# A seven-product form for the down projection of a decoder block, on one core

## The chip, the core and the metric

One Trainium2 chip; the kernel runs on one of its NeuronCores. The metric is the device time of one execution in microseconds, lower is better. In the text PE is TensorE, DVE is VectorE, ACT is ScalarE, POOL is GpSimd and SP is SyncE; POOL and SP issue DMA transfers here.

## The reference

One hybrid block over 528 tokens (16 learned meta tokens and 512 of the input, of which the last 512 are returned): attention and a state-space layer beside each other, an output projection with residual, then a dense feed-forward and a final norm. The part that the change touches, with 2048 features and 5632 = 44 x 128 hidden features:

```
m = rms_norm(h, norm_ffn)
h = h + (silu(m @ w_ffn_gate) * (m @ w_ffn_up)) @ w_ffn_down
out = rms_norm(h, norm_final)
```

All data are float32.

## The kernel before

Activations are held transposed, features on the 128 partitions and tokens along the free dimension. A float32 product runs as three float32r passes: every operand is split into a rounded high part and the remainder, and hi x hi + hi x lo + lo x hi is accumulated in PSUM. So each 128 x 128 weight tile costs three matmuls for each stretch of tokens. `hilo` (L299) makes the two parts, the high one by a copy on ScalarE, the low one by a subtraction on VectorE.

**Weights** come from DRAM in blocks of eight tiles (128 x 1024, 512 KB), loaded on SP's queue by `Weights.load` (L188), and are split in `_split` (L229) in the order of `_items` (L152). An item "P" is a plain block, "S" a unit of the seven-product form, "K" a block that stays in SBUF. `use` (L261) hands out the parts of item i after it has put the splits up to item i + 2 and the combinations (`_combine`, L210) up to item i + 3 into the queues of ScalarE and VectorE. High and low parts have three buffers each.

**Gate and up** are computed for 22 pairs of hidden tiles. Pair 0 is plain (`halves0`, L1275). For pairs 1 to 21, `seven` (L1339) computes two output tiles from 16 K tiles of one matrix as a two-by-two block product (halves of K, of the 512 tokens, and of the pair) in seven units P1, P5, P6, P2, P7, P3, P4 in place of eight. A unit is 8 K tiles x 3 passes = 24 matmuls of 256 columns. Four of the seven weight blocks are combinations made on VectorE, the sums among the products accumulate in the PSUM banks Ra (P1, P6, P7, P4), Rb (P5, P3) and Rc (P2); a unit that continues in a bank starts after the value of the unit before was read from it. The operands of the units are XD (P1), T12 (P5, P6), XA (P2, P3) and T34 (P7, P4); two quartets, gate into Cg and up into Cu, make a pair. Behind a pair VectorE multiplies Cu by Cg (L1397), for pairs 20 and 21 also by the token factor r_h (L1399), and POOL stores it to the DRAM tensor `ad` (L1400).

**Down** has 16 output tiles of 44 K tiles, in three parts of 20, 20 and 4 K tiles (`CHUNKS`, L41). In the first two, `down` (L1405) runs for each output tile 20 x 3 matmuls of 512 columns over streamed plain blocks; the operands are fetched from `ad` on POOL's queue (`fetch`, L1317) into other places, and split from there (`part`, L1331) behind units of the last quartet of gate and up and behind matmuls of the first output tiles. The first part is copied to SBUF (L1474); behind the second, VectorE adds, multiplies by r_h and adds the residual from `hd` (L1478 to L1480). The third part uses weights that stay, for each half of the tokens (L1504 to L1517), between the sums of squares of the final norm; `finish` (L1484) scales and stores.

Each engine works through its queue in the order in which the program issues: a VectorE or ScalarE instruction that waits holds up what is behind it, and so does a DMA issue on POOL or SP.

Of the kernel before, what the change touches and what calls it, by code (L numbers as in the profile page):

```python
# [12 lines left out]
"""  # L13
# [9 lines left out]
F32 = mybir.dt.float32  # L23
# [17 lines left out]
CHUNKS = (range(0, 20), range(20, 40), range(40, 44))  # L41
# [110 lines left out]
def _items():  # L152
    """What the projections take, in order: plain blocks, or (quartet, unit) of the seven-product form."""
# [4 lines left out]
    for q in range(2, 2 * NPAIR):  # L158
        it += [("S", q, u) for u in range(7)]
    d = N_PLAIN + N_GU  # L160
    return it + [("P", d + b) for b in range(80)] + [("K", d + 80 + b, KEEP[b]) for b in range(8)]


class Weights:
    """Weight blocks in the order of their use: loaded ahead, combined, split into hi and lo, handed out."""
# [6 lines left out]
    def __init__(self, nc, pool, ap):  # L172
# [15 lines left out]
    def load(self, upto):  # L188
        """Loads of the items before upto, as far as their places are free."""
# [13 lines left out]
    def _kept(self, tag, i):  # L203
        """The places of a block that stays."""
# [74 lines left out]
def _emit(nc, sp, pp, dp, A, out):  # L279
# [39 lines left out]
    # DRAM scratch  # L319
# [30 lines left out]
    def dense(X, nk, outs):  # L350
        """outs: (psum, first column, last column) of the same weights."""
# [38 lines left out]
    # ------------------------------------------------------------ input norm  # L390
# [52 lines left out]
    # ------------------------------------------------------------ u  # L443
# [873 lines left out]
    def fetch(f, tag, n_=2):  # L1317
# [4 lines left out]
        for i in range(n_):  # L1322
            staged[f + i] = t[:, i, :SEQ]
# [214 lines left out]
```

## Time and profile before

| | |
|---|---|
| Median of 3 runs | 2855.18 us (2852.67 to 2855.69) |
| Span of the profiled execution, first to last instruction | 2849.6 us |
| PE busy | 2816.9 us, 99% of the span |
| VectorE busy | 1668.6 us, 59% |
| ScalarE busy | 1063.2 us, 37% |
| Mean granted TensorE clock | 0.997 of full speed |
| DMA, mean | 120 GB/s, 341 MB |

The profiled execution's own time stands beside the others only as its span; it is 5.6 us (0.2%) under the median of the runs. Times in the rows below are in us from the span's start. Gate and up run to 2341 us, the down stage to 2836 us. A busy time is an engine's own; a row of a timeline merges equal instructions in succession, and an engine's next instruction can start shortly before the record of the one before ends.

### The profile page before, as it was taken

Reading aid. Unit: us, or ns where it says so; the run is one execution under the profiler, and the core shown is the slowest. Engines: PE = TensorE matmul, PEld = TensorE weight load, DVE = VectorE, ACT = ScalarE, POOL = GpSimd, SP = SyncE. Lnnn points to the kernel's source line nnn. Section 1 sums busy time; section 2 is a strip of 40 time slices with the busy share of each in tenths; the row PEclk is TensorE's granted clock in tenths of the full one; section 3 lists DMA queues with packets and bytes.
Section 4 is the critical chain, followed back from the end, with each engine's and each line's share of the span. In section 5 each row is a group of like instructions: output and inputs, shape, how many; then the busy total and the mean of one; then the engine's idle time right before and its main releaser. Section 6 shows DMA issues by size and latency. Waiting matters only on the chain.

```text
span 2849.6 us, 43701 instructions
## 1 busy us (share of the span) xinstructions
PE 2816.9 (99%) x18134; PEld 2524.0 (89%) x18134; DVE 1668.6 (59%) x2262; ACT 1063.2 (37%) x1549; POOL 342.4 (12%) x513
## 2 busy tenths in 40 slices
PE   9999999999999999999999999999999999999997
PEld 8988888889999788888889999999999998888887
DVE  6467457456666433343577777777777783224335
ACT  5223222235555332232344444444444452222124
POOL 2011221221111000111212000000000010000002
PEclk9999999999999999999999999999999999999999
DMA  5344454452222343334434333333333344334332
GB/s 190 105 116 121 126 144 112 132 138 79 68 67 60 115 144 108 114 115 147 138 107 148 122 123 113 125 124 122 119 119 119 134 173 138 96 111 143 108 113 94
DMA packets 103607, 341.41 MB, mean 120 GB/s; under 512 B 14800, under 2 KB 19664, under 8 KB 103344
## 3 DMA queue, kind: packets, MB, share of 16 engines
q1 hardware_dynamic: 76672, 263.36, 28.7%
q0 software_dynamic: 25312, 72.05, 8.7%
q10 hardware_dynamic: 1424, 3.21, 0.5%
q8 instruction: 142, 2.33, 0.3%
q14 instruction: 57, 0.47, 0.1%
HBM read 297.68 MB, written 33.10 MB: 116 GB/s over the span
## 4 chain that ended last, share of the span: by engine, by line
PE 94%; DVE 2%; ACT 1%; issue 1%; DMA 1%; POOL 0%; DVEq 0%; SPq 0%; ACTq 0%; POOLq 0%
PE psA L297 59%; PE psB L297 24%; PE psQ L297 5%; PE psV L297 4%; PE psD L297 2%; DVE ev L304 0%; DVE wlo L244 0%; ACT whi L243 0%; PE psA L1005 0%; DVE H L304 0%; DVE S L301 0%; POOL yd L739 0%; DVE S L304 0%; DMA H<-in_xT 0%; PE psQ L1005 0%
## 5 line engine op out<-in xcount | busy, mean ns | idle before, releaser
L297 PE MATMUL psA<-S,whi 128*128 128x512 f32 (+2 forms) x4960 | 1266.9, 340 | 8.6 <-ACT whi L243 6.3
L297 PEld LDWEIGHTS psA<-S,whi 128*128 128x128 f32 x4960 | 859.1, 188 | 123.3 <-ACT whi L243 6.3
L244 DVE TENSOR_TENSOR wlo<-raw,whi 128x1024 fp32r<-128x1024 f32 (+1 forms) x479 | 592.8, 1239 | 562.1 <-ACT whi L243 560.2
L297 PE MATMUL psA<-S,wlo 128*128 128x512 f32 (+2 forms) x2480 | 841.3, 339 | 0.1
L243 ACT ACTIVATE whi<-raw 128x1024 fp32r<-128x1024 f32 (+1 forms) x479 | 503.9, 1054 | 672.4 <-PE psA L297 324.0
L297 PEld LDWEIGHTS psA<-S,wlo 128*128 128x128 f32 x2480 | 466.8, 188 | 55.3 <-DVE wlo L244 0.5
L297 PE MATMUL psB<-S,whi 128*128 128x256 f32 (+2 forms) x1488 | 353.1, 312 | 0.1
L297 PEld LDWEIGHTS psB<-S,whi 128*128 128x128 f32 x1488 | 255.1, 189 | 17.6 <-PE psD L297 0.3
L297 PE MATMUL psB<-S,wlo 128*128 128x256 f32 (+2 forms) x744 | 231.1, 311 | 0.0
L244 DVE TENSOR_TENSOR wlo<-cmb,whi 128x1024 fp32r<-128x1024 f32 x126 | 154.5, 1226 | 82.5 <-ACT whi L243 82.5
L243 ACT ACTIVATE whi<-cmb 128x1024 fp32r<-128x1024 f32 x126 | 133.0, 1055 | 77.6 <-DVE wlo L244 69.9
L297 PEld LDWEIGHTS psB<-S,wlo 128*128 128x128 f32 x744 | 140.4, 189 | 8.3
L1400 POOL DMA_DIRECT2D ad<-sC x21 | 15.1, 718 | 775.2 <-DVE sC L304 693.8
L817 ACT ACTIVATE ev<-ev 128x512 f32<-128x512 f32 x32 | 20.2, 632 | 151.3 <-DVE ev L304 151.2
L297 PE MATMUL psA<-H,whi 128*128 128x264 f32 (+1 forms) x296 | 73.1, 337 | 1.0 <-DVE ev L304 1.0
L304 DVE TENSOR_TENSOR H<-psA,ev 128x512 f32<-128x512 f32 x32 | 22.1, 691 | 84.9 <-PE psA L297 84.9
L304 POOL TENSOR_TENSOR acc<-acc,ev 128x512 f32<-128x512 f32 (+2 forms) x43 | 53.3, 1240 | 131.3 <-ACT ev L1500 49.7
L301 DVE TENSOR_TENSOR S<-psA,S 128x512 fp32r<-128x512 f32 (+2 forms) x73 | 41.6, 575 | 42.3 <-ACT S L300 42.0
L304 DVE TENSOR_TENSOR ev<-ev,psA 128x512 f32<-128x512 f32 (+1 forms) x18 | 11.9, 659 | 91.0 <-POOL ev L304 88.3
L1368 ACT ACTIVATE ev<-psA 128x256 f32<-128x256 f32 x84 | 31.9, 380 | 86.3 <-PE psA L297 86.3
L297 PE MATMUL psB<-ssA,whi 128*128 128x256 f32 (+1 forms) x276 | 63.7, 319 | 0.0
L297 PE MATMUL psB<-T,whi 128*128 128x256 f32 (+1 forms) x276 | 63.7, 318 | 0.0
(571 smaller groups left out, 4639.3 us busy)
## 6 DMA issues: line engine op xcount, KB each, us to landing
raw<-in_wst SPq DMA_DIRECT2D x485, 512.0 KB, 3.6
ad<-sC POOLq DMA_DIRECT2D x21, 512.0 KB, 3.2
sg<-ev POOLq DMA_DIRECT2D x32, 256.0 KB, 2.3
ev<-sg POOLq DMA_DIRECT2D x32, 256.0 KB, 3.0
H<-ad POOLq DMA_DIRECT2D x11, 512.0 KB, 6.4
U<-ER POOLq DMA_DIRECT2D x64, 64.0 KB, 2.0
ev<-in_xT POOLq DMA_DIRECT2D x16, 256.0 KB, 3.0
hd<-H POOLq DMA_DIRECT2D x16, 256.0 KB, 2.3
```

Of the source, the lines that this page charges most:

```text
L243: self.nc.scalar.activation(hi[:, a:b], w[:, a:b], AF.Copy)
L244: self.nc.vector.tensor_tensor(lo[:, a:b], w[:, a:b], hi[:, a:b], op=ALU.subtract)
L297: PE.matmul(o, lhsT=l, rhs=r, start=start, stop=stop, skip_group_check=more)
L301: DVE.tensor_tensor(lo, src, hi, op=ALU.subtract)
L304: eng.tensor_tensor(o, a, b, op=op)
L817: ACT.activation(e, e, AF.Sigmoid)
L1368: ACT.activation(snap[name], o, AF.Copy)
L1400: POOL.dma_start(ad[2 * pr:2 * pr + 2].rearrange("f p n -> p f n"), Cu)
```

## The change

The token factor r_h is applied to every pair in gate and up, and the four token-side combinations of a pair, which the down projection needs as T12 and T34, are made there (`products`) and stored in a DRAM tensor `td` with the activations. The down projection then takes K tiles 0 to 15, 16 to 31 and 32 to 39 as three parts in the seven-product form (halves of K are even and odd tiles), and the tiles 40 to 43 as before, with weights that stay. In the first two parts the first pair of output tiles is plain (`plain_pair`), the other seven pairs are quartets of seven units; the third part takes four output tiles a quartet, with 4 K tiles and two groups of columns in a unit. The results of units are added straight from PSUM to a buffer C (`added`) that was loaded with the residual (first part) or the partial sum (others), and C goes back to DRAM (`pd`); in the third part it stays in SBUF. The operand tiles of a part are loaded as float32 into their final place and split in place (`begun`, `split`); `change` says behind which unit or plain block each kind is loaded and split, in the last quartet of the part before, the plain pair and the first quartet. The lists of items, the order of weights in DRAM and the tags of the weights that stay follow. Comments are also taken out.

```diff
-CHUNKS = (range(0, 20), range(20, 40), range(40, 44))
+DCH = (range(0, 16), range(16, 32), range(32, 40))
+LAST = range(40, 44)
...
+N_DOWN = (32, 32, 16)
-KEEP = ("ssB", "ER", ("S8", "S9"), ("S10", "S11"), ("S12", "S13"), ("S14", "S15"), ("v", "w"), ("U", "KS"))
+KEEP = ("ER", ("v", "w"), ("S0", "S1"), ("S2", "S3"), "ssA", "ssB", ("S8", "S9"), ("S10", "S11"))
...
-    return it + [("P", d + b) for b in range(80)] + [("K", d + 80 + b, KEEP[b]) for b in range(8)]
+    for c, n in enumerate(N_DOWN):
+        for q in range(n // 4):
+            if q == 0 and c < 2:
+                it += [("P", d + b) for b in (0, 2, 1, 3)]
+            else:
+                it += [("S", d + 4 * q, u) for u in range(7)]
+        d += n
+    return it + [("K", d + b, KEEP[b]) for b in range(8)]
...
+    def products(pr, Cu, T12_, T34_):
+        POOL.dma_start(td[pr, 0:2].rearrange("f p n -> p f n"), Cu)
+        if pr >= LAST.start // 2:
+            return
+        a, b = Cu[:, 0], Cu[:, 1]
+        tt(T12_[:, lo_], a[:, hi_], a[:, lo_], SUB)
+        tt(T34_[:, lo_], b[:, hi_], a[:, hi_], SUB)
+        tt(T12_[:, hi_], b[:, hi_], T12_[:, lo_], SUB)
+        tt(T34_[:, hi_], b[:, lo_], T12_[:, hi_], SUB)
+        POOL.dma_start(td[pr, 2], T12_)
+        POOL.dma_start(td[pr, 3], T34_)
...
+        tt(a, a, r_h, MUL)
+    products(0, Cu, ev(SEQ), ev(SEQ))
...
+    def added(C, nm):
+        def done(name, o):
+            for n_, m, c in {"P1": ((0, 0, lo_),), "P2": ((0, 0, lo_),), "P5": ((0, 1, hi_),), "P7": ((0, 1, hi_),),
+                             "P6": ((0, 0, hi_),), "P3": ((0, 0, hi_),), "P4": ((0, 1, lo_),)}[name]:
+                t = C[m][:, :, c]
+                tt(t, t, o.rearrange("p (m n) -> p m n", m=nm), ADD)
+        return done
+    def begun(tag, part, src, pair=None):
+        t = slot(tag, part)
+        if pair is None:
+            POOL.dma_start(t[:, 1].bitcast(F32), src)
+            return t
+        POOL.dma_start(t[:, 1].bitcast(F32).rearrange("p (k n) -> p k n", k=2), src.rearrange("k p n -> p k n"))
+        return t
+    def split(t):
+        ACT.activation(t[:, 0], t[:, 1].bitcast(F32), AF.Copy)
+        tt(t[:, 1], t[:, 1].bitcast(F32), t[:, 0], SUB)
...
+    def change(N):
+        L, S = (lambda kind, *k: lambda: N.load(kind, k)), (lambda kind, *k: lambda: N.split(kind, k))
+        if N.n == 8:
+            last = {"P1": [L("XD", 0, 1, 2, 3)],
+                    "P6": [S("XD", 0, 1, 2, 3), L("B12", 0, 1, 2, 3), L("T12", 0, 1, 2, 3)],
+                    "P7": [S("B12", 0, 1)],
+                    "P3": [S("B12", 2, 3), L("XA", *range(8))],
+                    "P4": [S("XA", 0), L("T34", *range(8))]}
+            plain = [[S("XA", 1, 2, 3, 4)], [S("XA", 5, 6, 7), L("T12", 4, 5, 6, 7)],
+                     [S("T12", 0, 1, 2, 3), S("T34", 0)], [S("T12", 4, 5, 6, 7)]]
+            first = {"P1": [S("T34", 1, 2, 3)], "P5": [S("T34", 4, 5)], "P6": [S("T34", 6)], "P2": [S("T34", 7)]}
+        else:
+            last = {"P1": [L("XD", 0, 1)],
+                    "P6": [S("XD", 0, 1), L("T12", 0, 1, 2, 3)],
+                    "P7": [S("T12", 0, 1)],
+                    "P3": [S("T12", 2, 3), L("XA", 0, 1, 2, 3)],
+                    "P4": [L("T34", 0, 1, 2, 3)]}
+            plain = None
+            first = {"P1": [S("XA", 0, 1, 2, 3)], "P5": [S("T34", 0, 1)], "P6": [S("T34", 2, 3)]}
+        return last, plain, first
...
-        if 2 * pr >= CHUNKS[2].start:
-            tt(Cu, Cu, rb, MUL)
-        POOL.dma_start(ad[2 * pr:2 * pr + 2].rearrange("f p n -> p f n"), Cu)
+        tt(Cu, Cu, rb, MUL)
+        products(pr, Cu, Cg[:, 0], Cg[:, 1])
+    def preload(c, m):
+        t = sb([P, 2, SEQ], F32, ("H7", "sC")[m % 2])
+        POOL.dma_start(t, (hd, pd[0])[c][2 * m:2 * m + 2].rearrange("k p n -> p k n"))
+        cbuf[c, m] = t
+    for c in range(2):
+        N = parts[c]
+        nxt_last = changes[c + 1][0]
+        for m in range(8):
...
+            if m == 0:
...
+                for j, o in enumerate(plain_pair(N.X, plain)):
+                    tt(C[:, j], C[:, j], o, ADD)
+            else:
+                hooks = {k: list(v) for k, v in (changes[c][2] if m == 1 else nxt_last if m == 7 else {}).items()}
+                hooks["P1"] = hooks.get("P1", []) + pre
+                C = cbuf.pop((c, m))
+                seven(N.X, 8, 1, added([C[:, 0:1], C[:, 1:2]], 1), hooks)
+            POOL.dma_start(pd[c][2 * m:2 * m + 2].rearrange("k p n -> p k n"), C)
...
+    N = parts[2]
+    hload(0)
+    hload(1)
+    for q in range(4):
+        hooks = {k: list(v) for k, v in (changes[2][2] if q == 0 else {}).items()}
+        if q == 0:
+            hooks["P3"] = [act_load]
+        elif q == 2:
+            for i, n_ in enumerate(("P1", "P6", "P7", "P4")):
+                hooks[n_] = [lambda i=i: act_split(i)]
+        if q < 3:
+            hooks.setdefault("P2", []).extend([lambda: hload(2 * q + 2), lambda: hload(2 * q + 3)])
+        seven(N.X, 4, 2, added(h2s[2 * q:2 * q + 2], 2), hooks)
```

`hload` loads two tiles of the second part's sums from `pd` into the places where the result stays; `act_load` and `act_split` do for the tiles 40 to 43 what `begun` and `split` do; `plain_pair` runs four plain blocks, the first two over XD and B12 (48 matmuls of 256 columns each), the others over XA (24 of 512). Loads of XD and B12 take 256 of the 512 columns of two tiles.

## Rows read from the trace of the kernel before

**Rows 1.** The page's head: the span, and for each engine busy us, share of the span and number of instructions.

```profile
span 2849.6 us, 43701 instructions
PE 2816.9 (99%) x18134; PEld 2524.0 (89%) x18134; DVE 1668.6 (59%) x2262; ACT 1063.2 (37%) x1549; POOL 342.4 (12%) x513
```

**Rows 2.** All waits of PE from 1290 us (output projection) to 2340 us (end of gate and up): us in total, times, longest.

```profile
PE psD L297 <- ACT whi L243: 0.8, 1, 0.8
PE psD L297 <- DVE wlo L244: 0.8, 1, 0.8
PE psA L297 <- DVE sC L304: 0.6, 1, 0.6
```

**Rows 3.** The table by stretch: from, to, length; busy us (and instructions) of each engine; granted clock; mean share of the DMA engines; GB/s. The first stretch is one pair of gate and up, the second the start of the down stage, the third the rest of its first part, the fourth most of its second part.

```profile
2224.00:2263.30 39.30, 39.30 (x338) 39.30 (x338) 30.58 (x31) 18.10 (x23) 0.72 (x1) 1.00 0.36 121
2341.00:2380.00 39.00, 39.00 (x170) 31.50 (x169) 19.88 (x24) 15.24 (x23) 6.60 (x11) 1.00 0.71 257
2380.00:2564.00 184.00, 184.00 (x793) 148.72 (x792) 48.39 (x47) 49.40 (x60) 2.05 (x4) 1.00 0.32 100
2640.00:2787.00 147.00, 147.00 (x636) 118.86 (x635) 51.95 (x56) 30.56 (x29) 4.31 (x8) 1.00 0.35 111
```

**Rows 4.** The chain that ended last, merged: start, us, engine, tile, instructions. The same step of two quartets of the seven-product form, with twelve between them.

```profile
1786.87 5.65 PE psA L297 x48
...
2042.45 5.64 PE psA L297 x48
```

**Rows 5.** PE's timeline (start, us of the merged run, engine, line, operation, tiles, count): the first matmuls of the down stage and the first of its last part.

```profile
2340.87 0.64 PE L297 MATMUL psA<-v,whi 128*128 128x512 f32 x2
...
2786.85 0.76 PE L297 MATMUL psA<-T,keep 128*128 128x256 f32 x5
```

**Rows 6.** PE's timeline in the last part: the first and the last of seven runs of six matmuls in a row.

```profile
2798.95 0.87 PE L297 MATMUL psA<-ssA,keep608S 128*128 128x256 f32 x6
...
2803.21 0.88 PE L297 MATMUL psB<-ssA,keep609S 128*128 128x256 f32 x6
```

**Rows 7.** VectorE's timeline (in brackets: idle time before it and what ended it): behind the first pair of gate and up, behind pair 19 and behind pair 20.

```profile
1516.27 2.49 DVE L304 TENSOR_TENSOR S<-H,S 128x512 fp32r<-128x512 f32 x4
1518.68 1.22 DVE L244 TENSOR_TENSOR wlo<-cmb,whi 128x1024 fp32r<-128x1024 f32 x1
...
2263.14 1.22 DVE L244 TENSOR_TENSOR wlo<-cmb,whi 128x1024 fp32r<-128x1024 f32 x1
...
2301.32 1.23 DVE L304 TENSOR_TENSOR sC<-sC,H 128x1024 f32<-128x1024 f32 x1 [0.56 <-ACT sC L1376]
2302.58 1.23 DVE L304 TENSOR_TENSOR sC<-sC,rstd 128x1024 f32<-128x1024 f32 x1
2303.72 1.22 DVE L244 TENSOR_TENSOR wlo<-cmb,whi 128x1024 fp32r<-128x1024 f32 x1
2304.86 1.22 DVE L224 TENSOR_TENSOR raw<-raw,raw 128x1024 f32<-128x1024 f32 x1
```

**Rows 8.** VectorE's timeline in the last part: additions from PSUM (512 and 256 columns), and at the end two operations of 256 of which the second needs the first.

```profile
2787.05 0.69 DVE L304 TENSOR_TENSOR H<-H,psB 128x512 f32<-128x512 f32 x1 [9.52 <-PE psB L297]
...
2791.39 0.41 DVE L304 TENSOR_TENSOR H<-H,psA 128x256 f32<-128x256 f32 x1
2791.72 0.41 DVE L304 TENSOR_TENSOR H<-H,psB 128x256 f32<-128x256 f32 x1
...
2836.80 0.89 DVE L304 TENSOR_TENSOR ev<-ev,S 128x256 f32<-128x256 f32 x2 [0.48 <-ACT S L384]
```

**Rows 9.** The timeline of PE's weight loads: the first low part of P6 behind the first pair and behind pair 20.

```profile
1520.07 0.19 PEld L297 LDWEIGHTS psA<-S,wlo 128*128 128x128 f32 x1
...
2306.47 0.19 PEld L297 LDWEIGHTS psA<-S,wlo 128*128 128x128 f32 x1
```

**Rows 10.** VectorE's timeline in the last quartet of gate and up: a pair of splits, and the addition of P7.

```profile
2333.51 1.28 DVE L301 TENSOR_TENSOR S<-wraw,S 128x512 fp32r<-128x512 f32 x2
...
2337.39 0.41 DVE L304 TENSOR_TENSOR sC<-ev,psA 128x256 f32<-128x256 f32 x1
```

**Rows 11.** PE's timeline there: the first matmuls of P4.

```profile
2337.94 0.48 PE L297 MATMUL psA<-S,whi 128*128 128x256 f32 x2 [0.60 <-DVE sC L304]
```

**Rows 12.** POOL's timeline at the start of the down stage: two issues of loads, of 512 and of 256 KB.

```profile
2352.60 0.72 POOL L1321 DMA_DIRECT2D sC<-ad  x1 [1.64 <-DMA ad<-sC]
2353.32 0.56 POOL L1321 DMA_DIRECT2D acc<-ad  x1
```

**Rows 13.** DMA issues: tiles, queue, operation, count, KB each, median us from issue to landing.

```profile
H<-ad POOLq DMA_DIRECT2D x11, 512.0 KB, 6.4
...
sC<-ad POOLq DMA_DIRECT2D x5, 512.0 KB, 4.2
```

**Rows 14.** The table by stretch, columns as in rows 3, in three stretches of 5 us at the start of the down stage.

```profile
2340.00:2345.00 5.00, 5.00 (x27) 4.24 (x26) 4.96 (x7) 3.23 (x6) 1.43 (x2) 1.00 1.01 395
2345.00:2350.00 5.00, 5.00 (x23) 4.02 (x23) 5.00 (x9) 4.30 (x7) 2.15 (x3) 1.00 1.02 395
2350.00:2355.00 5.00, 5.00 (x23) 4.05 (x22) 3.52 (x4) 1.06 (x1) 3.10 (x6) 1.00 0.99 360
```

More of the change, by code (lines that the diff above doesn't have):

```diff
@@ L324, in _emit @@
     hd = dp.tile([KT, P, SEQ], F32, name="hd")
-    ad = dp.tile([NFT, P, SEQ], F32, name="ad")
+    td = dp.tile([NPAIR, 4, P, SEQ], F32, name="td")
+    pd = [dp.tile([KT, P, SEQ], F32, name=f"pd{i}") for i in range(2)]
     gv = sb([P, 56], F32, "gv")
@@ L1328, in _emit @@
-    STAGE = {0: "wraw", 2: "wraw", 4: "wraw", 6: "H0", 8: "H1", 10: "H2", 12: "H6", 14: "H3", 16: "H0", 18: "H1",
-             20: "H2", 22: "H6", 24: "H3", 26: "H0"}
-    def part(f):
-        acts[f] = slot(*slots[f % 28])
-        hilo(acts[f][:, 0], acts[f][:, 1], staged.pop(f))
-        st.done.add(("act", f))
-        if f in range(7, 18, 2):
-            fetch(f + 9, STAGE[f + 9])
-    def seven(C, last):
-        Ra, Rb, Rc = ps([P, 512], "A")[:, :H2], ps([P, 512], "B")[:, :H2], None
-        snap = {}
-        for u, name in enumerate(UNITS):
+    X = {"XD": XD, "XA": XA, "T12": T12, "T34": T34}
@@ L1361, in seven @@
-            if last:
-                for f in PART.get(name, ()):
-                    part(f)
-                for f in FETCH.get(name, ()):
-                    fetch(f, STAGE[f])
+            for m in range(nm):
+                om = o[:, m * H2:(m + 1) * H2]
+                for k in range(nk):
+                    c = (m * nk + k) * P
+                    wh, wl = hi[:, c:c + P], lo[:, c:c + P]
+                    x = X["XD"][k // 2][:, :, k % 2] if name == "P1" else \
+                        X[{"P5": "T12", "P6": "T12", "P7": "T34", "P4": "T34"}.get(name, "XA")][k]
+                    if name != "P1":
+                        x = x[:, :, hi_ if name in ("P3", "P6", "P4") else lo_]
+                    start = m == k == 0 and name in ("P1", "P5", "P2")
+                    mm(om, wh, x[:, 0], start, False, True)
+                    mm(om, wh, x[:, 1], False, False, True)
+                    mm(om, wl, x[:, 0], False, k == nk - 1, True)
@@ L1366, in seven, with gathered @@
+            for h in hooks.get(name, ()):
+                h()
+            done(name, o)
+        seven_n[0] += 1
+    def gathered(C):
+        snap = {}
+        def done(name, o):
             if name in ("P1", "P5", "P6"):
@@ new lines, in _emit, with __init__, load, split @@
+    class Operands:
+        def __init__(self, c):
+            self.i0, self.n = DCH[c].start // 2, len(DCH[c]) // 2
+            self.raw, self.X = {}, {n: [None] * self.n for n in ("XA", "T12", "T34")}
+            self.X["XD"], self.X["B12"] = [None] * (self.n // 2), [None] * (self.n // 2)
+        def load(self, kind, ks):
+            for k in ks:
+                i = self.i0 + (2 * k if kind in ("XD", "B12") else k)
+                if kind in ("XD", "B12"):
+                    tag, part = (NX[8 + k] if kind == "XD" else (f"S{4 + k}", 0))
+                    t = begun(tag, part, td[i:i + 2, 0][:, :, lo_ if kind == "XD" else hi_], 2)
+                else:
+                    tag, part = {"XA": NX[k], "T12": (f"S{k}", 0), "T34": (f"S{8 + k}", 0)}[kind]
+                    t = begun(tag, part, td[i, {"XA": 1, "T12": 2, "T34": 3}[kind]])
+                self.raw[kind, k] = t
+        def split(self, kind, ks):
+            for k in ks:
+                t = self.raw.pop((kind, k))
+                split(t)
+                self.X[kind][k] = k2(t) if kind in ("XD", "B12") else t
@@ L1379, in _emit @@
     seven_n = [0]
-    PART = {"P5": range(0, 2), "P6": range(2, 4), "P2": range(4, 6), "P7": range(6, 8), "P3": range(8, 10),
-            "P4": range(10, 12)}
-    FETCH = {"P6": (8, 10), "P2": (12,), "P7": (14,)}
+    parts = [Operands(c) for c in range(3)]
+    changes = [change(N) for N in parts]
     rb = r_h.unsqueeze(1).to_broadcast([P, 2, SEQ])
@@ L1391, in _emit @@
         Cu = sb([P, 2, SEQ], F32, "sC")
[L1392 to L1405 removed]
+        seven(X, 8, 1, gathered(Cu), changes[0][0] if pr == NPAIR - 1 else {})
@@ new lines, in _emit, with hload, act_load, act_split @@
+    hs_, h2s = [], []
+    def hload(j):
+        t = sb([P, 2, SEQ], F32, f"S{(4, 5, 6, 7, 12, 13, 14, 15)[j]}")
+        POOL.dma_start(t, pd[1][2 * j:2 * j + 2].rearrange("k p n -> p k n"))
+        h2s.append(t)
+        hs_.extend([t[:, 0], t[:, 1]])
+    acts, begun_ = {}, {}
+    def act_load():
+        for i, f in enumerate(LAST):
+            begun_[f] = begun(*NX[(6, 7, 10, 11)[i]], td[f // 2, f % 2])
+    def act_split(i):
+        f = LAST[i]
+        split(begun_[f])
+        acts[f] = begun_[f]
@@ L1406, in down @@
+    def down(fs, ot, c, w):
         p = ps([P, 512], "AB"[ot % 2])
```

161 lines of the change are left out of this document (59 added, 102 removed).

## The prediction

> **What bounds the kernel now.** The page's list of busy times comes first: PE is busy 99% of the span, VectorE 59%, ScalarE 37% [rows 1]. A busy PE is not yet a PE that nothing holds up, so the waits of PE come next: from the output projection to the end of gate and up (1,050 us) three waits, 2.2 us together [rows 2]. The table by stretch then tells what each stage does beside PE: gate and up keep VectorE busy 30.58 of 39.3 us, the down stage only 48.39 of 184 us; the granted clock is 1.00 (2.4 GHz) in both, and DMA is used to a third [rows 3]. So the kernel ends when PE has pushed its columns through; VectorE in gate and up has some 8 us of slack in a pair of products, and in the down stage much.
>
> Two paces give the prices. Units of the seven-product form repeat on the chain of waits every 19.66 us: 13 periods from 1786.87 to 2042.45, each of 168 matmuls of 256 columns, 117.0 ns apiece [rows 4]. A unit of 24 is then 2.81 us. The first two parts of the down stage run from 2340.87 to 2786.85, 445.98 us for 32 output tiles of 60 matmuls of 512 columns: 13.94 us a tile, 232.3 ns a matmul [rows 5].
>
> **The gain.** Those two parts hold 40 K tiles by 16 output tiles. After the change they are 20 blocks of 16 K tiles by two output tiles (or 8 by four): 2 in plain form, 18 in seven products. A plain pair now costs 96 matmuls of 256 and 48 of 512 columns, 96 x 117.0 + 48 x 232.3 ns = 22.38 us; a seven costs 19.66. 18 x 19.66 + 2 x 22.38 = 398.6 us, **47.3 us less** than 445.98. Sevens of the third part use chains of four K tiles; the trace has chains of four in the last stage, 36 matmuls from 2798.95 to 2803.21, 118.3 ns [rows 6]. The ends are 117.0 and 118.3, at most 0.9 us over 672 matmuls; I take 117.0, since the seven's order of operands is kept.
>
> The Trainium skill (TensorE: Matmul & The Clock Gate, section "Wait — 56ns, not 53.3ns?") gives a warm matmul N / 2.4 GHz plus about 2.5 ns, a fixed cost that speaks against more and shorter matmuls. By it, 109.2 and 215.8 ns, an estimate, a seven would save 2.4 us in place of 2.6 and the gain would be 42.6 us. The rows show 117.0 and 232.3 ns, so the measured overhead grows with the columns, and the rows decide.
>
> **What is added beside PE.** In a seven of the down stage VectorE has 7 low parts and 4 combinations, which start 1.14 us apart back to back [rows 7], and 7 additions from PSUM of 0.41 us [rows 8]: at most 2.70 us in a unit, 15.4 of 19.66. It fits in 2.81, so I cost it at nothing. In the third part the additions are 512 wide, 0.69 us [rows 8]: 2.97 us in four units and 1.83 in three, 17.4 in all, which the slack of two units ahead takes up. Without that cover each addition would stand on the path, 2.9 us a quartet. Weight blocks are as many as before, on SP's queue; stores and reloads of partial sums add 1 MB a quartet on POOL's, which only issues there. The three additions and multiplications per output tile of the old second part were hidden [rows 3] and return nothing.
>
> **Where stalls come in.** (a) *Products in each pair.* Behind Cu, VectorE now multiplies by the token factor and takes four differences before the low part that the next quartet's P6 wants. Pair 20 shows the multiplication already: Cu*Cg at 2301.32, the factor at 2302.58, low part at 2303.72 [rows 7]. Small operations of 256 start 0.33 apart when independent and 0.45 when one needs the other [rows 8]: first difference at 2303.84, the others at 2304.17, 2304.50 and 2304.95, low part at 2305.28, done 2306.50. PE loads that low part at 2306.47 [rows 9], and a signal takes 0.1: PE resumed at 2337.94 after an addition from 2337.39 that lasted 0.41 [rows 10, 11]. So 0.14 us a pair, 19 pairs: **2.7 us**; ends 0 and 0.45 a pair, 8.5 us. POOL's three stores come behind it and gate Cg's place only at the next P2, 8 us on.
> (b) *First pair.* There the low part for P6 follows four splits at 1516.27 and ends at 1519.90 [rows 7], PE wants it at 1520.07 [rows 9]. One factor (0.7) and four differences (1.5) come ahead: 2.2 - 0.17 + 0.1 = **2.1 us**, ends 0 and 3.
> (c) *Gate and up into the first part.* Before, 12 tiles were split in that last quartet (two of 0.64 us a unit [rows 10]), and PE waited 0.6 [rows 11]. Now nine are, with loads one unit or more ahead, but the copy of P6 stands behind four splits on ScalarE. I put 1.0 in place of 0.6: **0.4**. The plain pair follows, with two weight blocks already split (11 us), so a late XA0 holds VectorE and not PE. The same cover serves the step from the first part to the second. In each first seven VectorE has seven splits more, 15.4 + 7 x 0.6 = 19.6 us: I get 0.2 late at P7, **0.4** for both.
> (d) *Second part into the third.* No plain pair here. POOL issues four T34 loads behind P4 (0.56 each), the store of C and then the first two loads of partial sums (0.72 each [rows 12]): the first is issued 2.96 us after P4. A 512 KB load landed 6.4 us after issue in the crowded stretch and 4.2 outside [rows 13]; the crowd is nearer. It lands at 9.4, VectorE adds P1 by 10.1, and P6, which accumulates into that bank, starts at 10.2 where it wanted 5.6: 4.6 us. Behind that addition stand two combinations, two low parts, four splits and two additions, 8.3 us, to 18.4; P7 needs the last at 15.8: 2.7 more. **7.3 us**; with 4.2 it is 5.1, with all landed early 0, with a landing two us later 10.
>
> **Sum.** -47.3 + 2.7 + 2.1 + 0.4 + 0.4 + 7.3 = -34.4 us. On the profiled span, 2849.6, that gives 2815.2. The runs' median, 2855.18, lies 5.6 above that span and carries what surrounds it; I leave that difference as it is: **2820.8 us**.
>
> **The rivals.** *Covers hold.* The steps (a) to (d) cost under 6 us: 2808 to 2814. For it: PE lost only 0.6 us in the old change of operands, which split more tiles in a quartet [rows 10, 11]. Against: no old step put a load from DRAM in front of an addition that PE waits for.
> *Transfers too slow at the full changes.* A full change fetches 32 tiles of 256 KB (8.4 MB), half of those for XD and B12 in rows of 1 KB, beside weights of 100 GB/s [rows 3] and 1.6 MB of partial sums. XD's 1.0 MB comes early; from P6 of one quartet to P7 of the quartet behind the plain pair PE has some 42 us for the rest: 7.4 + 1.6 + 4.2 = 13.2 MB, 314 GB/s. At a full DMA share the trace moved 360 to 395 GB/s [rows 14], which suffices; 257, the mean of the old change [rows 3], would take 51 us, 9 late at each of two changes: 2839.
> The Trainium skill (DMA: Bandwidth & Descriptors, section "Where 436 GB/s comes from") puts a core's share of HBM at about 358 GB/s. The rows passed it here, 395 GB/s; by 358 the bytes would still fit, an estimate of 37 us.
> *The chain of products has no cover: slower.* If the factor and the four differences (1.26 + 1.56 = 2.82 us) were wholly on the path of each pair, 19 x 2.82 = 53.6 us in place of 2.7: 2872. It decides from 2.4 us a pair. For it: VectorE runs without a gap from Cu to that low part [rows 7]. Against: the low part was ready 2.8 us early in pair 19 (2263.14 + 1.22 against 2267.15, a period before 2306.47) and 1.5 early in pair 20, and 0.14 is what is left of it.
> *The third part gains nothing.* Its quartets take the plain time (short chains, wide additions): 4 x 2.6 = 10.5 us back, 2831.
>
> **How the numbers follow.** Forecast 0.55 (2814 to 2828), covers hold 0.15, slow transfers 0.20, no gain in the third part 0.04, chain without cover 0.06. The predicted time is the forecast's. The range runs from 2808 (covers hold) to 2841 (slow transfers), and leaves out the slower case and some of both tails. About 0.2%, 5.7 us, is what a measurement tells from no change: faster takes the first four cases but for 0.02 of the slow transfers that would end near 2855; slower is the chain.
>
> **What would show it.** Right: sevens of 19.7 us in the down stage, the matmuls' last stage beginning some 34 us earlier in all, pairs of gate and up at 39.3 to 39.5 us, a PE wait on VectorE at P6 and P7 in the first quartet of the third part, DMA near full share at three places. Wrong: pairs above 40 us (a), sevens above 20.5 us in the middle of a part (additions on the path), PE waiting on ScalarE or VectorE for splits in a plain pair (transfers), or a granted clock below 1.00 in the down stage, which would mean that waits are longer than reckoned.

## The result and the profile after

The changed kernel takes **2831.2 us** (median of 4 runs, 2828.9 to 2832.3) against 2853.9 for the kernel before beside it: ratio 0.992, 95% interval 0.9906 to 0.9934, 22.7 us less. Forecast were 2820.8 (34.4 less) in a range of 2808 to 2841. The profiled spans differ by 19.3 us, 2849.6 and 2830.3. The head of the page, answering to [rows 1]: PE 35 us less, VectorE 240 us more.

```profile
span 2830.3 us, 47269 instructions
PE 2781.7 (98%) x19526; PEld 2566.1 (91%) x19526; DVE 1908.8 (67%) x2609; ACT 1136.6 (40%) x1625; POOL 413.5 (15%) x633
```

Starts of stages, from PE's timeline (start, us, engine, line, operation, tiles, count), in this order: pairs 20 and 21 of gate and up, its last quartet; the plain pair, the first and the second seven of part 1; the same three of part 2; the first two quartets of part 3; the last part.

```profile
2265.35 0.40 PE L314 MATMUL psA<-v,whi 128*128 128x256 f32 x2
...
2304.80 0.28 PE L314 MATMUL psA<-v,whi 128*128 128x256 f32 x1
...
2324.46 0.40 PE L314 MATMUL psA<-v,whi 128*128 128x256 f32 x2
...
2344.12 0.40 PE L314 MATMUL psA<-v,whi 128*128 128x256 f32 x2
...
2366.71 0.40 PE L314 MATMUL psA<-v,whi 128*128 128x256 f32 x2
...
2395.73 0.40 PE L314 MATMUL psA<-v,whi 128*128 128x256 f32 x2
...
2513.99 0.40 PE L314 MATMUL psA<-v,whi 128*128 128x256 f32 x2
...
2536.57 0.39 PE L314 MATMUL psA<-v,whi 128*128 128x256 f32 x2
...
2565.60 0.40 PE L314 MATMUL psA<-v,whi 128*128 128x256 f32 x2
...
2683.56 0.40 PE L314 MATMUL psA<-v,whi 128*128 128x256 f32 x2
...
2709.68 0.40 PE L314 MATMUL psA<-v,whi 128*128 128x256 f32 x2
...
2768.50 0.88 PE L314 MATMUL psA<-T,keep 128*128 128x256 f32 x6
```

A pair of gate and up lasts 39.45 us (39.32 before), its last quartet 19.66. The plain pairs last 22.59 and 22.58 us (2344.12 to 2366.71, 2513.99 to 2536.57). The sevens in the middle of a part last 19.66: from 2395.73 to 2513.99 it is 118.26 for six, 0.3 over six times that. But the first sevens of parts 1 and 2 last **29.02 and 29.03** (2366.71 to 2395.73, 2536.57 to 2565.60), and the first quartet of part 3 lasts 26.12. In what PE waited for in the down stage, those three stand out (PE's timeline, the wait in brackets; P6 of the first sevens, then P6 in part 3):

```profile
2379.47 0.77 PE L314 MATMUL psA<-S,whi 128*128 128x256 f32 x2 [4.05 <-DVE sC L321]
2548.71 0.77 PE L314 MATMUL psA<-S,whi 128*128 128x256 f32 x2 [4.03 <-DVE sC L321]
2693.05 0.77 PE L314 MATMUL psA<-S,whi 128*128 128x256 f32 x2 [3.70 <-DVE S L321]
```

Each wait is followed by slow matmuls. The table by stretch (columns as in rows 3) for the first change of operands and the seven behind it:

```profile
2345.00:2370.00 25.00, 25.00 (x167) 22.84 (x167) 17.33 (x22) 10.83 (x17) 8.11 (x14) 1.00 1.02 392
...
2370.00:2375.00 5.00, 3.66 (x21) 2.48 (x19) 2.22 (x4) 2.76 (x5) 0.00 (x0) 1.00 0.32 125
2375.00:2380.00 5.00, 0.95 (x4) 0.77 (x5) 5.00 (x8) 3.63 (x7) 0.90 (x2) 0.72 0.28 105
2380.00:2385.00 5.00, 5.00 (x29) 5.00 (x28) 5.00 (x7) 2.00 (x3) 0.56 (x1) 0.59 0.69 202
2385.00:2390.00 5.00, 5.00 (x44) 5.00 (x43) 4.63 (x7) 2.22 (x3) 0.00 (x0) 1.00 0.34 112
```

DMA is at full share for 25 us, at 392 GB/s; [rows 14] had 360 to 395 for 15 us. Then PE stands, and in the 5 us after the wait the granted clock is 0.59, near the lower of its two levels (1.2 GHz, the other is 2.4): 29 matmuls in place of 44. So the 9.4 us that the first seven of part 1 is too long are three things: P5 ends 3.1 us late, PE waits 4.05 us for P6, and P6 takes 2.3 us longer than elsewhere. What PE stood for is read backwards. VectorE's timeline (start, us, ..., in brackets the idle time before):

```profile
2359.34 1.23 DVE L241 TENSOR_TENSOR cmb<-raw,raw 128x1024 f32<-128x1024 f32 x1 [5.31 <-DMA raw<-in_wst]
2360.48 1.22 DVE L261 TENSOR_TENSOR wlo<-raw,whi 128x1024 fp32r<-128x1024 f32 x1
2361.61 3.09 DVE L321 TENSOR_TENSOR S<-S 128x512 fp32r<-128x512 f32 x5
...
2374.17 0.69 DVE L321 TENSOR_TENSOR S<-S 128x512 fp32r<-128x512 f32 x1 [0.77 <-ACT S L1413]
2374.78 0.68 DVE L321 TENSOR_TENSOR H<-H,psA 128x512 f32<-128x512 f32 x1
2375.38 0.68 DVE L321 TENSOR_TENSOR H<-H,psB 128x512 f32<-128x512 f32 x1
2375.97 1.22 DVE L261 TENSOR_TENSOR wlo<-cmb,whi 128x1024 fp32r<-128x1024 f32 x1
2377.11 1.89 DVE L321 TENSOR_TENSOR S<-S 128x512 fp32r<-128x512 f32 x3
2378.92 0.41 DVE L321 TENSOR_TENSOR sC<-sC,psA 128x256 f32<-128x256 f32 x1
```

The addition of P1 at 2378.92, which P6 waits for, stands behind three T34 splits, a low part, the sums of the plain pair and the last T12 split at 2374.17. That split waited for ScalarE, and ScalarE for four landings:

```profile
2368.22 0.63 ACT L1413 ACTIVATE S<-S 128x512 fp32r<-128x512 f32 x1 [6.02 <-DMA S<-td]
2370.73 0.63 ACT L1413 ACTIVATE S<-S 128x512 fp32r<-128x512 f32 x1 [1.88 <-DMA S<-td]
2372.04 0.63 ACT L1413 ACTIVATE S<-S 128x512 fp32r<-128x512 f32 x1 [0.67 <-DMA S<-td]
2373.51 0.63 ACT L1413 ACTIVATE S<-S 128x512 fp32r<-128x512 f32 x1 [0.84 <-DMA S<-td]
```

Those are T12 4 to 7. POOL issued them behind the XA loads, which begin at 2339.68, behind all eight T34 loads (the fifth of them at 2349.22), a store and a load of a buffer C (POOL's timeline, T12 4 to 7 last):

```profile
2339.68 1.07 POOL L1407 DMA_DIRECT2D ssA<-td  x2 [2.31 <-PE psB L314]
...
2349.22 1.20 POOL L1407 DMA_DIRECT2D S<-td  x2 [2.25 <-DMA ER<-td]
...
2356.02 0.57 POOL L1407 DMA_DIRECT2D S<-td  x1 [0.78 <-PE psB L314]
2356.82 0.55 POOL L1407 DMA_DIRECT2D S<-td  x1 [0.24 <-issue]
2358.13 0.54 POOL L1407 DMA_DIRECT2D S<-td  x1 [0.76 <-DMA S<-td]
2359.59 0.54 POOL L1407 DMA_DIRECT2D S<-td  x1 [0.92 <-DMA S<-td]
```

Their places S4 to S7 hold B12 until the second block of the plain pair has read it, but tile by tile, and the issues come 3.8 to 4.6 us after that: the block's matmuls on the four tiles of B12 end at 2351.4, 2352.9, 2354.3 and 2355.7. POOL was still at what stands ahead in its queue; the view's `PE psB` at 2356.02 is the last semaphore to move, not the end of that place's use (experiment 1 shows the same issues coming as each place falls free). P5 begins at 2369.5 (2366.71 + 2.81) and wants the last of them 21 matmuls later, at 2372.0; its split ends at 2374.9.

In part 3 the addition of P1 itself stands, for the partial sums:

```profile
2692.22 0.69 DVE L321 TENSOR_TENSOR S<-S,psA 128x512 f32<-128x512 f32 x1 [3.15 <-DMA S<-pd]
```

Other steps. Behind pair 19 VectorE now runs (answering to [rows 7]):

```profile
2265.96 1.23 DVE L321 TENSOR_TENSOR sC<-sC,H 128x1024 f32<-128x1024 f32 x1 [0.56 <-ACT sC L1390]
2267.22 1.23 DVE L321 TENSOR_TENSOR sC<-sC,rstd 128x1024 f32<-128x1024 f32 x1
2268.48 0.76 DVE L321 TENSOR_TENSOR H<-sC 128x256 f32<-128x256 f32 x2
2269.16 0.88 DVE L321 TENSOR_TENSOR H<-sC,H 128x256 f32<-128x256 f32 x2
2269.95 1.22 DVE L261 TENSOR_TENSOR wlo<-cmb,whi 128x1024 fp32r<-128x1024 f32 x1
```

The low part is done at 2271.2, and the first low matmul of P6 behind it starts 2271.23. On the chain of waits, P6 behind a pair takes 2.94 us, P6 in the middle of a pair 2.83 (start, us, engine, tile, instructions):

```profile
1541.48 2.83 PE psA L314 x24
...
1561.14 2.94 PE psA L314 x24
```

### The profile page after: what moved, and what is told of

Its sections match the earlier page's. It is cut to its first block, busy times and chain, and to the rows that moved or that the text cites. A ratio compares the mean times of both kernels' runs of the same rounds, so it can differ in the third digit from the quotient of the medians.

```text
span 2830.3 us, 47269 instructions
## 1 busy us (share of the span) xinstructions
PE 2781.7 (98%) x19526; PEld 2566.1 (91%) x19526; DVE 1908.8 (67%) x2609; ACT 1136.6 (40%) x1625; POOL 413.5 (15%) x633
## 3 DMA queue, kind: packets, MB, share of 16 engines
q10 hardware_dynamic: 1424, 3.21, 0.5%
## 4 chain that ended last, share of the span: by engine, by line
PE 92%; DVE 3%; DMA 3%; issue 1%; ACT 1%; POOL 0%; DVEq 0%; SPq 0%; POOLq 0%; ACTq 0%
PE psA L314 60%; PE psB L314 19%; PE psQ L314 6%; PE psV L314 5%; DMA S<-td 2%; PE psD L314 1%; DVE S L321 1%; DVE wlo L261 1%; DVE ev L321 0%; PE psA L1023 0%; ACT whi L260 0%; DMA ER<-td 0%; DMA H<-in_xT 0%; PE psQ L1023 0%; PE psB L678 0%
## 5 line engine op out<-in xcount | busy, mean ns | idle before, releaser
L314 PE MATMUL psA<-S,whi 128*128 128x256 f32 (+2 forms) x5472 | 1317.9, 328 | 20.5 <-DVE sC L321 8.1
L314 PEld LDWEIGHTS psA<-S,whi 128*128 128x128 f32 x5472 | 930.8, 189 | 119.1 <-ACT S L1413 8.5
L314 PE MATMUL psA<-S,wlo 128*128 128x256 f32 (+2 forms) x2736 | 896.9, 328 | 2.6 <-DVE wlo L261 2.6
L314 PE MATMUL psB<-S,whi 128*128 128x256 f32 (+1 forms) x1424 | 293.5, 284 | 2.4 <-DVE S L321 1.4
L261 DVE TENSOR_TENSOR wlo<-cmb,whi 128x1024 fp32r<-128x1024 f32 x180 | 219.8, 1221 | 68.4 <-ACT whi L260 67.3
L314 PE MATMUL psB<-S,wlo 128*128 128x256 f32 (+1 forms) x712 | 200.3, 281 | 0.0
L241 DVE TENSOR_TENSOR cmb<-raw,raw 128x1024 f32<-128x1024 f32 x60 | 73.1, 1219 | 11.4 <-DMA raw<-in_wst 11.4
L241 DVE TENSOR_TENSOR cmb<-cmb,raw 128x1024 f32<-128x1024 f32 x60 | 73.2, 1219 | 0.0
L241 DVE TENSOR_TENSOR raw<-raw,raw 128x1024 f32<-128x1024 f32 x60 | 73.1, 1218 | 0.0
L241 DVE TENSOR_TENSOR cmb<-raw,cmb 128x1024 f32<-128x1024 f32 x60 | 73.1, 1218 | 0.0
```

The costliest lines, as they stand in the source:

```text
L241: self.nc.vector.tensor_tensor(t, g(a), g(b), op=op)
L261: self.nc.vector.tensor_tensor(lo[:, a:b], w[:, a:b], hi[:, a:b], op=ALU.subtract)
L314: PE.matmul(o, lhsT=l, rhs=r, start=start, stop=stop, skip_group_check=more)
```

## Experiments

Theory A: at a full change DMA is full, T12 4 to 7 are issued last on POOL's queue and land last, and everything behind their splits is late. B: VectorE has too much to do in a first seven. C: the bytes are too many in whatever order. Diffs are against the changed kernel, for the last five against the kernel named. Lengths of the three slow stages are in the table behind.

**1. T34 4 to 7 behind T12 4 to 7.**

```diff
-"P4": [S("XA", 0), L("T34", *range(8))]}
+"P4": [S("XA", 0), L("T34", 0, 1, 2, 3)]}
-[S("XA", 5, 6, 7), L("T12", 4, 5, 6, 7)],
+[S("XA", 5, 6, 7), L("T12", 4, 5, 6, 7), L("T34", 4, 5, 6, 7)],
```

> Changed kernel, but T34's tiles 4 to 7 are loaded behind T12's tiles 4 to 7 (after the second plain block) and not before them. Theory A (T12 4 to 7 land late because they stand behind eight T34 loads in POOL's queue while DMA is full, and ScalarE and VectorE wait for them in order): the first seven of parts one and two falls from 29.0 us to 20 to 24 us each, the kernel to 2813 to 2822 us. Theory B (VectorE has too much to split and add in a first seven): 28 to 29.5 us each, no change. Theory C (too many bytes in the window, whatever their order): now T34 comes late, 27 to 30 us each.

2824.1 us. First sevens 23.0 and 24.7 us in place of 29.0: 10.3 us come back with the same bytes and the same work. That is A. Of the 10.3 us, 8.2 come back before P6 begins and 4.4 in P6, which now runs at the full clock; 2.2 go again at P7. Waits of 1.67 and 1.17 us stay in the first, 3.40 and 1.16 in the second. POOL now issues T12 4 to 7 as their places fall free, one tile of B12 after the other (its timeline; the last row has two T34 loads with T12 7):

```profile
2353.98 0.57 POOL L1407 DMA_DIRECT2D S<-td  x1 [1.80 <-PE psB L314]
2355.41 0.55 POOL L1407 DMA_DIRECT2D S<-td  x1 [0.86 <-PE psB L314]
2356.85 0.54 POOL L1407 DMA_DIRECT2D S<-td  x1 [0.88 <-PE psB L314]
2358.26 1.60 POOL L1407 DMA_DIRECT2D S<-td  x3 [0.87 <-PE psB L314]
```

Counted from the start of the plain pair (2346.37 here, 2344.12 in the changed kernel) they are issued 3.5 to 4.3 us earlier and land 4.9 to 6.1 us earlier. So most of the gain is an earlier issue, the rest a shorter way from issue to landing.

**2. T34 of parts 1 and 2 not fetched.** The old tiles are split again, so P7 and P4 of those parts multiply old operands.

```diff
+ if kind == "T34" and self.n == 8:
+     self.raw[kind, k] = (parts[0].X if self.i0 else X)["T34"][k]
+     continue
```

> Changed kernel without the reload of T34 in parts one and two: its old tiles are split again in place, so all work of ScalarE, VectorE and PE stays and 4 MB of transfers go (the products with T34 then have old operands). Theories A and C: first sevens of 19.7 to 21 us in place of 29.0, the kernel near 2812 us. Theory B: 28 to 29.5 us, no change.

2819.5 us; first sevens 22.2, where 19.7 to 21 was forecast, and 20.3. With 2 MB less to fetch in each change and every split still there, 2.5 and 0.7 us over 19.66 remain: B can't be more than that.

**3. First two loads of partial sums for part 3 behind P2** of the last quartet of part 2.

```diff
+ if c == 1 and m == 7:
+     hooks["P2"] = hooks.get("P2", []) + [lambda: hload(0), lambda: hload(1)]
...
-    hload(0)
-    hload(1)
     for q in range(4):
```

> Changed kernel, but the first two loads of partial sums for the third part are issued behind P2 of the last quartet of part two, not behind the T34 loads. Theory (the addition of P1 waits for that load): the first seven of part three falls from 26.1 us to 20 to 22 us, the kernel by 4 to 6 us. Rival (the splits of XA and T34 in front of the additions hold PE): 25 to 26 us, no change. The first sevens of parts one and two stay at 29.0 us.

2825.6 us. The first quartet of part 3 lasts 23.1 in place of 26.1, at a clock of 1.00; the wait at P6 fell from 3.70 to 0.67 us, and a second one of 2.33 us at P7, which waits for VectorE's addition of P6, took its place. So step (d) had both its mechanisms; in the changed kernel the second was covered by slow matmuls. The 23.1 lies between the two forecasts. And of the 5.6 us less in the whole the edit itself accounts for 3.0: the first sevens of parts 1 and 2 come before it and last 27.4 and 27.8 here. That is how far one profile of the same code can differ from another; experiment 4 has 28.1 and 27.4. Against those, experiment 1 gained 7.5 and 7.8 us in place of 10.3.

**4. Products of a pair behind P1 of the next pair.**

```diff
-        seven(X, 8, 1, gathered(Cg), {})
+        seven(X, 8, 1, gathered(Cg), {"P1": [lambda: products(pr - 1, Cu, Cg[:, 0], Cg[:, 1])]})
...
-        products(pr, Cu, Cg[:, 0], Cg[:, 1])
```

> Changed kernel, but stores and differences of a pair are issued behind P1 of the next pair's gate quartet, so behind the low part for P6 (the factor stays where it is). Theory (a low part that comes 0.14 us late in each pair, 2.6 us late in the first): pairs of gate and up fall from 39.44 to 39.32 us, the first quartet of pair 1 from 24.0 to 19.7 to 20.7 us, the kernel by 5 to 7 us. Rival (the work only moves on and meets the next low part or the additions): pairs stay at 39.4 us or more, the kernel within 2 us.

2830.4 us, where 5 to 7 less was forecast. Pairs last 39.32 in place of 39.45, so step (a) is shown, and the first quartet of pair 1 lasts 20.1; but pair 1 begins 5.7 us later in this profile than in the changed kernel's, and 2.4 us are less than one run can tell in the whole.

**5. Additions ahead of the splits.**

```diff
+            done(name, o)
             for h in hooks.get(name, ()):
                 h()
-            done(name, o)
```

> The changed kernel with one swap: in every unit the value of the unit is read (the addition into C) before the splits that the unit's hook issues, in place of behind them. Loads and their order stay. Theory A with VectorE's order (late T12 tiles, and then three T34 splits of 1.9 us in VectorE's queue ahead of the addition of P1 that P6 waits for): the last T12 split is as late as before, but the wait at P6 shrinks from 4.05 us to some 2.1, and if the granted clock then stays at 1.00 the 2.5 us of slow matmuls go too: first sevens of parts 1 and 2 of 24.5 to 27.2 us each against 29.0, first quartet of part 3 by its four XA splits (2.7 us) from 26.1 to 22 to 24, the whole 2817 to 2825 us. Rival, landing alone: the splits wait for the landings whatever the order, first sevens stay at 28.5 to 29.5, 2829 to 2833. Rival, order made worse: an addition that waits for PE now holds up the splits behind it and P7 or P2 waits in turn: over 2833.

2831.7 us (2829.3 to 2833.7, 4 runs; ratio to before 0.992, 0.9908 to 0.9938): no gain. The waits at P6 did fall, from 4.05 and 4.03 to 2.25 each, and the first sevens to 26.5 and 27.7; but part 3's first quartet grew to 29.5, since the addition of P1, now first, waits for the partial sums and holds the XA splits behind it (4.35 us at P6, then 1.99 at P7, clock 0.66 after either). The rival of a worse order holds there, A's arithmetic in the first sevens.

**6. Edits 1, 3 and 4 together.**

> Three edits together: T34 4 to 7 loaded behind T12 4 to 7, the first two loads of partial sums for part 3 behind P2 of the last quartet of part 2, and the products of a pair issued behind P1 of the next pair. By the stretches measured one at a time against the changed kernel: first sevens 23.0 and 24.7 in place of 29.0 each (-10.3), first quartet of part 3 23.1 in place of 26.1 (-3.0), pairs 39.32 in place of 39.45 (19 x 0.13 = -2.4), first quartet after pair 0 20.1 in place of 24.0 (-3.9): -19.6, so some 2811.5 us (2808 to 2815). Rival (the gains overlap: VectorE or DMA that one edit relieves is what the other edit relied on): 2816 to 2822.

2818.0 us (2817.1 to 2822.0; ratio 0.9878, 0.9863 to 0.9892). It misses 2811.5: the first sevens keep their gain (23.3, 24.5), part 3 gives half (24.6, with the wait of 2.32 us followed by a clock of 0.71), and the 3.9 us on the first pair were not there to be had: five kernels that issue it as the changed one does waited 0.41, 0.41, 1.70, 2.15 and 2.58 us at that place. (This profile gains 4.1 us there, but its pair 1 begins 2.8 us later than the changed kernel's.) The trace shows what is left in the first seven: VectorE stands before the first combination, then runs without a gap.

```profile
2349.02 1.29 DVE L321 TENSOR_TENSOR T<-T 128x512 fp32r<-128x512 f32 x2
2356.10 1.23 DVE L241 TENSOR_TENSOR cmb<-raw,raw 128x1024 f32<-128x1024 f32 x1 [5.80 <-DMA raw<-in_wst]
```

So the weight blocks on SP's queue are late as well in the crowd, and with them the T12 splits that are queued behind the combination and were long landed.

**7. Edits 1, 3, 4 and 5.**

> The three edits of the run before and the values of units read before the hook's splits. If VectorE's order is what is left at P6 of the first sevens (1.67 us, and 3.40 at the second change) and at P7 of part 3 (2.33), those waits lose up to 1.9, 1.9 and 2.0 us: 2806 to 2809. If the landings alone set them: within 1.5 us of the run before.

2818.7 us (2818.4 to 2822.3; 0.9881, 0.9865 to 0.9898): as the run before, where up to 12 us less was forecast if VectorE's order were what is left. The first addition no longer waits for splits but for its buffer, `sC<-hd`, which POOL loads last of all (VectorE's timeline):

```profile
2371.29 0.42 DVE L321 TENSOR_TENSOR sC<-sC,psA 128x256 f32<-128x256 f32 x1 [1.55 <-DMA sC<-hd]
```

**8. As 7, all eight T34 loads behind T12 4 to 7.**

> As the run before, but all eight T34 tiles are loaded behind T12 4 to 7 and split behind the first seven's units. Theory A (order in POOL's queue with DMA full): the last T12 tiles land 4 loads (1 MB, 2.6 us at 395 GB/s) earlier, so the waits at P6 of both first sevens go, each seven 19.7 to 21 us, 1 to 4 us less than the run before. Theory C (the bytes do not fit): T34 lands too late in turn, P7 waits as long as P6 did, no gain or a loss of 1 to 3 us.

2820.2 us (2819.1 to 2821.5; 0.9883, 0.9868 to 0.9898): no gain. VectorE stands 3.21 us ahead of the same addition (1.55 in the run before), whose buffer is now loaded behind four more tiles (the view names no releaser; by the trace the buffer lands at 2373.85 and the addition starts at 2373.93), PE waits 2.69 at P6, and T34 is late in turn (0.95 and 0.96 at P7).

**9. As 6, T12 0 to 3 split a block earlier**, and T34 2 and 3 of part 3 split behind P2.

```diff
-[S("XA", 5, 6, 7), L("T12", 4, 5, 6, 7), ...
+[S("XA", 5, 6, 7), S("T12", 0, 1, 2, 3), L("T12", 4, 5, 6, 7), ...
-[S("T12", 0, 1, 2, 3), S("T34", 0)], ...
+[S("T34", 0)], ...
-"P5": [S("T34", 0, 1)], "P6": [S("T34", 2, 3)]}
+"P5": [S("T34", 0, 1)], "P2": [S("T34", 2, 3)]}
```

> The kernel with three edits (2818.0 us), and: the splits of T12 0 to 3 stand behind the second block of the plain pair in place of the third, and T34 2 and 3 of part 3 are split behind P2 in place of P6. In the three-edit kernel VectorE stands idle for 5.8 us behind the XA splits, until a weight block lands that the first combination of the first seven needs (DMA full), and then runs without a gap to the end of the first seven. Theory D (weights late on SP's queue hold VectorE's queue, and what is behind it is late by as much): the four splits (2.5 us) fall into that idle time, and the wait at P6 of the first seven (1.99 us) goes to 0.5 or less, first sevens 20.5 to 22 and 23 to 24.5, whole 2813.5 to 2816.5. Rival E (C of the first seven, loaded last on POOL's queue, lands just as late): P6 waits for that load in place of VectorE, first sevens as before within 0.7 us. Part 3: addition of P6 is 1.28 us earlier, wait at P7 2.32 down to 1.0 to 1.3.

2818.7 us (2817.3 to 2823.5; 0.9878, 0.9863 to 0.9893): no gain. The splits did fall into the idle time (3.14 left of 5.80), and the first seven is as long as before, since the addition of P1 now waits for the buffer C (0.96 us of the 1.86 that PE waits). The second is 1.0 us longer (25.4). Part 3 went as forecast: 22.8 in place of 24.6, a wait of 1.12 at P7 (and one of 0.58 in it). Rival E holds for the first seven:

```profile
2373.26 0.42 DVE L321 TENSOR_TENSOR sC<-sC,psA 128x256 f32<-128x256 f32 x1 [0.96 <-DMA sC<-hd]
```

**10. As 9, C of the first seven loaded ahead of T34 4 to 7.**

```diff
-                plain[2] += pre
+                plain[1][-1:-1] = pre
```

> As the run before, and the load of C for the first seven is issued ahead of T34 4 to 7. If rival E holds: the wait at P6 goes here, first sevens 20.0 to 21.5 and 22 to 23.5, 1.5 to 4 us less than the run before. If theory D alone holds: no change, or 1 us more because T34 6 and 7 land later.

2816.4 us (2814.4 to 2817.4; 0.9866, 0.9851 to 0.9881). First seven 22.0, wait at P6 0.67 in place of 1.86, as E has it. The second is no shorter (25.9), where 22 to 23.5 was forecast: there T12 4 to 7 land 12.2 to 12.9 us after their issue, their splits end at 2529.9, and 4 us of VectorE's work (sums of the plain pair, a low part, three T34 splits) stand between these and the addition of P1 at 2533.96. That is a wait of 3.37 us and a clock of 0.50 after it.

**11. As 10, all T34 loaded last, additions ahead of splits.**

> As the run before, but all eight T34 tiles are loaded last, and a unit's value is read before the hook's splits. At the second change T12 4 to 7 still landed 10 us after issue with T34 0 to 3 ahead of them (wait at P6 3.0). If order decides there: second first seven 21 to 22 in place of 23, whole up to 2 us less than the run before. If the bytes decide: T34 makes P7 and P4 wait 1 to 2.4 us, as in the earlier run with T34 last (0.25 and 0.95, 1.43 and 0.96), whole 0 to 2 us more.

**2813.5 us** (2811.8 to 2819.0; 0.986, 0.9844 to 0.9877), the lowest median, though its runs overlap with those of experiment 10 and the two profiled spans are both 2812.6. First sevens 20.9 and 21.6 us; these are two edits at once, and how much of the 4.3 us in the second is the order of the loads and how much that of the additions was not separated. What the sevens gain is in part lost elsewhere: 25.1 for 22.8 in the first quartet of part 3 (waits of 1.98 and 1.18 at P7, where additions ahead of splits had cost time in experiment 5 too) and 21.4 for 19.8 in that of pair 1. Of the waits in the first sevens three are left, 2.4 us in all (sum, times, longest):

```profile
PE psA L314 <- DVE S L321: 1.9, 2, 0.9
PE psA L314 <- DVE sC L321: 0.5, 1, 0.5
```

| kernel | first seven, part 1 | part 2 | first quartet, part 3 | us |
|---|---|---|---|---|
| changed | 29.0 | 29.0 | 26.1 | 2831.2 |
| 1 T12 first | 23.0 | 24.7 | 26.0 | 2824.1 |
| 2 no T34 | 22.2 | 20.3 | 26.5 | 2819.5 |
| 3 sums early | 27.4 | 27.8 | 23.1 | 2825.6 |
| 4 products later | 28.1 | 27.4 | 27.5 | 2830.4 |
| 5 additions first | 26.5 | 27.7 | 29.5 | 2831.7 |
| 6 = 1, 3, 4 | 23.3 | 24.5 | 24.6 | 2818.0 |
| 7 = 6 and 5 | 24.6 | 25.2 | 23.9 | 2818.7 |
| 8 T34 last | 25.9 | 25.1 | 22.4 | 2820.2 |
| 9 splits earlier | 23.2 | 25.4 | 22.8 | 2818.7 |
| 10 C ahead | 22.0 | 25.9 | 22.8 | 2816.4 |
| 11 C ahead, T34 last | 20.9 | 21.6 | 25.1 | 2813.5 |

Experiments 1 to 4 are one run each, beside one of 2854.6 for the kernel before.

Taken together: A holds, and what it says of T12 holds of the buffer C in turn. The bytes fit (sevens of 20.9 and 21.6 with all of them), so theories B and C together explain at most 1.2 and 1.9 us; the order of loads, splits and additions explains 8.1 and 7.4 of the 9.4 us that each first seven of the changed kernel's profile was too long, slow matmuls included. Each length in the table is from one profile, and the same code differs there by up to 1.6 us, so steps smaller than that between two rows tell little by themselves.

## Why the prediction was right and wrong

| step | forecast | profile |
|---|---|---|
| units in place of tiles | -47.3 | -46.8 |
| (a) products, 19 pairs | +2.7 | +2.4 |
| (b) first pair | +2.1 | +4.4 |
| (c) gate and up into part 1 | +0.4 | -0.9 |
| (c) two first sevens | +0.4 | **+18.7** |
| (d) part 2 into part 3 | +7.3 | +6.5 |
| last part | 0 | -0.9 |
| sum | -34.4 | -16.6 |

The sum of the right column and the span's -19.3 differ by 2.7 us, by which the first quartet of pair 1 begins earlier (1511.64 against 1514.30), behind code that is the same but for the multiplication by r_h in pair 0; in other runs of the changed code it began at up to 1517.8.

- **Gain**: sevens of 19.66, as [rows 4] have them; the plain pairs 0.2 longer than worked out, part 3's quartets 0.05 shorter. The Trainium skill (TensorE: Matmul & The Clock Gate, section "Wait — 56ns, not 53.3ns?") would have a seven save 2.4 us, an estimate; the trace shows 22.30 to 19.66, 2.6.
- **(a)** right to 0.02 us a pair, and for the reason given: the low part ends 0.1 late, P6 takes 2.94 for 2.83, and with the products elsewhere pairs are back at 39.32. So the slower rival (2872) is refuted: VectorE had the cover that two rows in [rows 7, 9] gave it. (By its own sum that rival decides from 2.25 us a pair, not 2.4.)
- **(b)** right in place: PE waits for that low part. The size changes from run to run; here the first quartet lasts 24.03 us (1511.64 to 1535.67), with a wait of 2.58 and slow matmuls behind it, elsewhere the wait was 0.41 to 2.15. How far the 2.1 of the forecast was right is therefore not told by one profile.
- **(c), the step that failed**: "the same cover serves the step from the first part to the second", and a first seven "0.2 late at P7". I counted VectorE's work (it is 2.5 us at most, experiment 2) and took the loads for landed. Against slow transfers I set bytes against rate: 13.2 MB in 42 us, 314 GB/s, at 360 to 395 enough. The rate was no shortage (392 for 25 us). The Trainium skill (DMA: Bandwidth & Descriptors, section "Where 436 GB/s comes from") puts a core's share of HBM at about 358 GB/s; this trace passes it again, with those 392. But an average over 42 us says nothing of the tile that is issued last: the places of T12 4 to 7 fall free from 2351.4 on, but the loads stand in POOL's queue behind 2 MB that nobody needs until P7, are issued 3.8 to 4.6 us late and land 12.2 to 13.9 us after that. So the "transfers too slow" rival, 9 us at each change and 2839 in all, had the size (9.4) and the place, but not the cause: not the rate of 257 in [rows 3], but the order. The time lies between the two cases, and inside the range because that reached to this rival, not because the forecast had its reason; the forecast itself is 10.4 us off.
- **(d)** 6.5 for 7.3. The wait at P6 was 3.70 for 4.6 forecast, and the first addition waited for the partial sums as said (3.15 us on `S<-pd`). The second stall, 2.7 at P7, hid behind slow matmuls and came out, 2.33 us, in experiment 3.
- **Half clock**: I named a clock below 1.00 as a sign that waits are longer than reckoned. They were: P6 took 5.1 to 5.5 us for its usual 2.8 after each of the three, 7.5 us that no term of the sum had.

## What to carry to other kernels

When a stage change fills the DMA engines, don't set bytes against rate alone: write down, in the order of the issuing queue, when each tile's place comes free and when its first reader starts, and price the last one that is issued and needed first. Loads that are wanted late should be issued late, and no load should stand behind one that is wanted later. That goes for the small ones too: after T12 was put right, the 512 KB buffer of the first addition was the next to be late. In an in-order engine, a wait for one late operand delays work that was ready; put splits that have landed ahead of a combination that may wait for its weights. Each such step here only uncovered the next wait (experiments 7 to 9 gained nothing by themselves), so look for the next one before pricing it.

## What was not expected of the hardware

- With DMA at full share, POOL no longer issues at its own pace. The first XA loads follow one another in 0.53 us; from 2356 on the issues are 0.8 to 1.5 us apart, and the view names a landing of another tile as the end of two of the waits. The trace tells which: POOL's transfers use eight semaphores (the counters that engines wait on) in turn, and each is issued only when the transfer eight before it has landed. None of the 508 of this trace is issued earlier, nor any in the traces of the other kernels, and the waits that the view puts down to that landing end 0.28 to 0.56 us after it. When a load takes 9 us to land, the ninth in a row is held up by the first. Whether more semaphores would help was not tried. So an early place in the queue counts twice: what stands behind is issued later, and then lands later.
- The granted clock fell near 0.5 to 0.7 after waits of 4 us, but not after each wait of the same length: 2.33 us at P7 in experiment 3 and 3.40 in experiment 1 left it at 1.00, 2.32 us at P7 in experiment 6 were followed by 0.71, and 1.94 us at P6 in experiment 7 by 0.61. What decides was not settled.
